# The low part of each weight tile by an accumulating transfer instead of a subtraction on VectorE

## The chip, the core and the metric

The kernel runs on one core of a Trainium2 chip. A core has engines that work side by side and each take their own instructions in order: TensorE (PE; its weight loads are shown as PEld), VectorE (DVE), ScalarE (ACT), GpSimd (POOL) and SyncE (SP), which here only starts transfers. Sixteen DMA engines move data between the main memory and the on-chip memory, and inside the latter. The metric is the time of one execution on the device in microseconds (us).

## The reference

One inference step of two layers for a prompt of 512 tokens and a sample of 64 tokens, 1024 features, all in float32. Layer 0 mixes by attention with forget gates and by a gated linear recurrence, layer 1 by a gated product over chunks of 128 tokens; each is followed by a feed-forward block of 2 x 2816 columns with a causal convolution of width 3. The products with weights are most of the work:

```
q, k, v, f, xb, gb = split(x @ w_in_e)            # 1024 x 2568
y = concat(attention(q, k, v, f), gelu(gb) * rg_lru(xb)) @ w_out_e
x = LN(ALPHA * x + y)
h = causal_dwconv(x @ ffn_w_up, ffn_conv_w)       # 1024 x 5632
g, u = split(h);  x = LN(ALPHA * x + (gelu(g) * u) @ ffn_w_down)
# layer 1: z = gelu(x @ w_in_o); u, v = split(z); y = (u * mixed(LN(v))) @ w_out_o; LN; the same FFN
```

## The kernel before

All 576 tokens stay on the chip, features on the partitions (`x`, eight blocks of 128). To multiply float32 values at the rate of float32r, a weight tile W and the activations X are each cut into a high part (the value rounded to float32r) and a low part (the rest), and each product is three matmuls: high x high, high x low, low x high (`triplet`, lines 293 to 295). The activations' parts are `xh`/`xl` or `hh`/`hl`.

The weights come as 188 tiles ("units", 128 partitions x up to 1040 columns, mostly 512 KB), in a fixed list. For each one, SP loads a raw tile (`raw`, four buffers, line 141). Then `split_part` makes the parts: ScalarE copies the raw tile into the high part (`whiA` or `whiB`, line 164), and VectorE subtracts high from raw into the low part (`wloA`/`wloB`, line 165). Pool A holds four units; pool B, which is open during the feed-forward blocks, four more. A unit is 8 blocks x 2 halves of the tokens x 3 = 48 matmuls, each with 288 columns.

The order of the work is written out by hand: no scheduler moves it. `need(units)` splits what is missing; after a unit's last matmul `retire` frees its slot and `pump(2)` splits up to two more units (`split_next`), and after each split the next raw load is issued (`dma_next`, at most four loads ahead). So in one engine's queue a split stands where the pump stands in the program, behind the evictions of the unit before it.

Three places differ from the steady stream:

- The start. The first two units are loaded and split in two pieces each, between the transposes of the input tokens (`x_in`, lines 511 to 513). POOL first starts 17 small loads (lines 247, 252, 528, 531).
- The ends of a mixer and of a feed-forward block (`tail_units`): the last four units run with one half of the tokens after the other, and pumps run inside the first half, while POOL and VectorE add up the sums for the layer norm (`Norm.acc`, lines 391 and 407; the statistics are matmuls at line 422). The next sublayer's first four units (`first_group`) follow.
- The token-major products (`v_sweep`, `vf_run`), where the weight is the moving operand and a unit is used up in a shorter time.

Of the kernel before, what the change touches and what calls it, by code (L numbers as in the profile page):

```python
# [22 lines left out]
AF = mybir.ActivationFunctionType  # L23
OP = mybir.AluOpType
# [31 lines left out]
def stream_step(ctx, tc, I, O):  # L56
    nc = tc.nc
    PE, ACT, DVE, POOL = nc.tensor, nc.scalar, nc.vector, nc.gpsimd
# [14 lines left out]
    x = big.tile([128, 8, T], FT, name="x")  # L73
    xh = big.tile([128, 8, T], FR, name="xh")
    xl = big.tile([128, 8, T], FR, name="xl")

# [1 line left out]
    units = []  # L78

    def wunit(w, off, ncols, c0, k0, nk, slot):  # L80
# [81 lines left out]
    def split_part(u, i):  # L162
        c = slice(u.parts[i][0] * u.width, u.parts[i][1] * u.width)
        ACT.activation(u.hi[:, c], u.raw[:, c], AF.Copy)  # L164
        DVE.tensor_sub(u.lo[:, c], u.raw[:, c], u.hi[:, c])  # L165

    def pump(n=1):
        for _ in range(n):
# [3 lines left out]
    def need(us):  # L172
        while any(u.hi is None for u in us):
            assert split_next()

    def retire(us):
        for u in us:
            live[u.slot] -= 1

# [1 line left out]
    later = []  # L181

    def defer(n, fn):
# [14 lines left out]
        while later:  # L198
            later.pop(0)[1]()

# [1 line left out]
    mones = consts.tile([128, 128], FT, name="mones")  # L202
    DVE.memset(mones, 1.0 / D)
    e0s, e0 = opened("ev0", side="left")
# [64 lines left out]
        nc.sync.dma_start(t[2], dram(s, l * 2 * 2 * DFF, [[128, 88], [1, 128]]))  # L269
        rowsF[l] = t  # L270

# [1 line left out]
    ps = {}  # L273

    def open_main():
        es, p = opened("psmain", side=None, space=bass.MemoryType.PSUM)
        ps["es"], ps["p"], ps["mm"] = es, p, ("mm", 6)
# [5 lines left out]
    def auxbank():  # L283
        return ps["p"].tile([128, 512], FT, name="aux", bufs=2)
# [31 lines left out]
    def seq(us, h, l, post, ks=None, hooks=None):  # L316
        for i, u in enumerate(us):
            need([u])
            for half in range(2):
                sweep([u], half, h, l, lambda _, hf, b, i=i: post(i, hf, b), ks=ks, hooks=hooks)  # L320
                hooks = None
            retire([u])
            pump(2)
# [14 lines left out]
        retire(us)  # L338
        pump(2)

# [1 line left out]
    lnp = {}  # L342

    class Norm:
        """Statistics of x = alpha * x + update about a per-token shift (the mean of the first 256 features)."""

        def __init__(self, g, b, first, halves=HALF, nb=96):
            self.g, self.b, self.first, self.halves, self.nb = g, b, first, halves, nb
# [126 lines left out]
                    at[2]: lambda: self.scale(half, 0, 4), at[3]: lambda: self.scale(half, 4, 8)}  # L475

    def tail_units(us, norm):
        """Output units 2..7 of a sublayer; the last four run one half of the tokens after the other."""
        seq(us[0:1], hh, hl, lambda i, hf, b: norm.post(2, hf, b), hooks={4: norm.shift})
        seq(us[-5:-4], hh, hl, lambda i, hf, b: norm.post(3, hf, b))  # L480
        us = us[-4:]
        need(us)
        post = lambda i, hf, b: norm.post(4 + i, hf, b)
        sweep(us, 0, hh, hl, post, hooks={c: pump for c in (3, 11, 19)})
        sweep(us, 1, hh, hl, post, hooks=norm.hooks(0))
        retire(us)
# [7 lines left out]
            retire(us[i:i + 2])  # L494
            pump(2)

    # =====================================================================
    # layer 0, even mixer
    # =====================================================================
    open_main()  # L500
    # the clock of TensorE rises after some microseconds of work: give it some while the first rows come in
    bk = auxbank()
    for _ in range(7):
        PE.matmul(bk[:, :128], mones, mones, start=True, stop=True)
# [43 lines left out]
    first = [E["xb0"], E["xb1"]]  # L548
# [18 lines left out]
    retire(first)  # L567
    pump(2)

    # per-channel vectors and the forget gates  # L570
    bk = auxbank()
    PE.transpose(bk[:, :112], rows0, ident[:112, :112])
    DVE.tensor_copy(vec, bk[:, :112])

    def log_sigmoid(z, w, name):
        """min(z, 0) - log(1 + e), e = exp(-|z|), the logarithm by the series of atanh(e / (2 + e)); z is overwritten."""
        e, t = e0.tile([128, w], FT, name=name + "e"), e0.tile([128, w], FT, name=name + "t")
        r = ev.tile([128, w], FT, name=name)
        DVE.scalar_tensor_tensor(e, z, -1.0, z, op0=OP.mult, op1=OP.max)
        ACT.activation(e, e, AF.Exp, scale=-1.0)  # L580
        DVE.tensor_scalar(t, e, 2.0, None, op0=OP.add)
        DVE.reciprocal(t, t)
        DVE.tensor_mul(e, e, t)
        DVE.tensor_mul(t, e, e)
        DVE.tensor_scalar(r, t, 1.0 / 19, None, op0=OP.mult)
        for d in (17, 15, 13, 11, 9, 7, 5, 3):
            DVE.scalar_tensor_tensor(r, r, 1.0 / d, t, op0=OP.add, op1=OP.mult)
        DVE.scalar_tensor_tensor(r, r, 1.0, e, op0=OP.add, op1=OP.mult)
        DVE.tensor_scalar(z, z, 0.0, None, op0=OP.min)
        DVE.scalar_tensor_tensor(r, r, -2.0, z, op0=OP.mult, op1=OP.add)  # L590
        return r
# [33 lines left out]
        seq([E[f"gb{j}"]], xh, xl, lambda _, hf, b: gb_post(j, hf, b))  # L625
        vecF_prep(j)

    # gates of the recurrence
    NXH = ((0, 290), (290, NX))
    for s, (dst, bias) in enumerate(((rr, "rg_ba"), (ii, "rg_bx"))):  # L630
        for j in range(4):
# [33 lines left out]
    for j in range(2, 4):  # L665
# [4 lines left out]
                p = 2 * (j - 2) + a  # L670
                PE.transpose(bk[:, 256 * a + 128 * t:256 * a + 128 * t + 128], ck[:, t, p * 128:(p + 1) * 128], ident)
        DVE.tensor_copy(ckT[:, 2 * j - 4:2 * j - 2, :], bk.rearrange("p (a c) -> p a c", a=2))
    # v, token-major
    vt = ev.tile([128, 5, 512], FT, name="vt")

    def v_sweep(us, post):
# [14 lines left out]
        for t in range(5):  # L691
            post(t, 128 if t < 4 else TS, banks[t])

    # the columns of v and of the forget gates lie side by side: two runs of 260
    lsz = e0.tile([128, 40], FT, name="lsz")
    DVE.memset(lsz, 0.0)

# [37 lines left out]
    nc.sync.dma_start(dram(O[3], 0, [[512, 128], [128 * 512, 4], [1, 512]]), vt[:, :4])  # L735
    nc.sync.dma_start(dram(O[6], 0, [[512, TS], [1, 512]]), vt[:TS, 4])

    # cumulative log forget values as rows: cached | new of the sample | prompt
    nb = e0.tile([8, 832], FT, name="nb")
    b0, b1 = auxbank(), auxbank()  # L740
    for t in range(4):
# [24 lines left out]
    def q_tiles(p):  # L766
        qh[p] = at.tile([128, TP - 128], FR, name="qh", bufs=3)
        ql[p] = at.tile([128, TP - 128], FR, name="ql", bufs=3)
# [7 lines left out]
        DVE.tensor_copy(kT[:, p, a:b], bk[:, :H2])  # L776

    def q_post(p, half, bk):
        """Scaled queries: the first tile of the prompt and the sample in float32, the rest as two float32r parts."""
        a, b = HALF[half]  # L780
        if half == 0:
            q_tiles(p)
        f0, f1 = (0, 128) if half == 0 else (TP, T)
        h0, h1 = (128, b) if half == 0 else (a, TP)
        hi, lo = qh[p][:, h0 - 128:h1 - 128], ql[p][:, h0 - 128:h1 - 128]
        ACT.activation(hi, bk[:, h0 - a:h1 - a], AF.Copy, scale=0.125)
        ACT.activation(qT[:, p, f0:f1], bk[:, f0 - a:f1 - a], AF.Copy, scale=0.125)
        DVE.scalar_tensor_tensor(lo, bk[:, h0 - a:h1 - a], 0.125, hi, op0=OP.mult, op1=OP.subtract)
# [41 lines left out]
    ats, at = opened("at", side="right")  # L830
# [4 lines left out]
    retire([E["k1"]])  # L835
    ps["es"].close()

# [1 line left out]
    aes, ap_ = opened("psatt", space=bass.MemoryType.PSUM)  # L839
    ps["p"], ps["mm"] = ap_, ("fil", 2)  # L840

# [190 lines left out]
    open_main()  # L1032
    tail_units(E["out"][2:8], n1)

    # =====================================================================
    # gated conv FFN
    # =====================================================================
    def ffn(layer, prev, norm):
        up, down = Fs[layer]
        V = vecF[layer]  # L1040
# [77 lines left out]
    wes["es"].close()  # L1118
    wpool["B"] = None

    # =====================================================================
    # layer 1, gated spatial mixing
    # =====================================================================
    oes, op = opened("odd", side="right")

    def u_post(m, half, bk):
# [113 lines left out]
    n4 = Norm(None, None, False, HALF4, 128)  # L1240
    dl = ffn(1, n3, n4)

# [1 line left out]
    fes, fp = opened("fin", side="right")  # L1244
    gB2 = fp.tile([128, D], FT, name="gB2")
    bB2 = fp.tile([128, D], FT, name="bB2")
# [123 lines left out]
```

## Time and profile before

| | |
|---|---|
| time, median of 2 runs | 1321.01 us (1320.17 to 1321.86) |
| profiled execution: span from first to last instruction | 1319.8 us; the profile tells no other time for it, so the runs stand beside the span |
| TensorE busy, matmul / weight load | 1290.8 us (98%) / 1256.0 us (95%) |
| VectorE, ScalarE, POOL busy | 768.4 us (58%), 483.1 us (37%), 398.2 us (30%) |
| granted TensorE clock, mean | 0.987 of full speed |
| transfers | 113.8 MB, 28.9% of the sixteen DMA engines' time on the hardware queue, 0.2% on the software queue |

A busy share is a mean over stages with different limits. Times are counted from the span's start. "Idle before, releaser" in a group means how long an engine sat idle ahead of such an instruction and what ended most of that. Instructions that only issue a transfer, wait or branch are not counted as busy, and SP's are shown as SPq.

### The profile page before, as it was taken

The numbers are of one execution on the slowest core, as the hardware profiler recorded it, in microseconds if no ns is written. First come the engines' busy times: TensorE is split into PE (matmuls) and PEld (weight loads), VectorE is DVE, ScalarE is ACT, GpSimd is POOL, SyncE is SP. The second block draws the span as 40 slices with busy tenths as digits, with TensorE's granted clock in tenths as the row PEclk, the third lists the DMA queues.
The fourth block names the chain that finished last, engine by engine and source line by source line (L and its number), as shares of the span: only waits on it lengthen the run. The fifth ranks groups of instructions, "written<-read, shape, count | busy, mean of one in ns | idle before, by whom it ended". The sixth has DMA issues, their size and how long they took to land. (4 is left out here: it accounts for less than half of the span.)

```text
span 1319.8 us, 23538 instructions
## 1 busy us (share of the span) xinstructions
PE 1290.8 (98%) x9567; PEld 1256.0 (95%) x9567; DVE 768.4 (58%) x1294; ACT 483.1 (37%) x936; POOL 398.2 (30%) x603
## 2 busy tenths in 40 slices
PE   8999999999999999999999998999999999999995
PEld 8999888999999999999999788999999999999995
DVE  4557777777543555355564348777653465445556
ACT  4553554445421332234334242444431233223331
POOL 3322222763200221022183025565320122012234
PEclk9999999999999999999999998999999999999997
DMA  9316221314232223322312412314323222322112
GB/s 234 113 33 199 79 84 41 97 47 144 83 96 80 74 74 94 97 75 71 94 38 68 139 50 73 96 33 128 113 80 96 78 66 81 97 86 64 43 36 72
DMA packets 192017, 113.80 MB, mean 86 GB/s; under 512 B 4221, under 2 KB 184733, under 8 KB 191909
## 3 DMA queue, kind: packets, MB, share of 16 engines
q1 hardware_dynamic: 191300, 111.95, 28.9%
q8 instruction: 75, 1.23, 0.4%
q0 software_dynamic: 608, 0.35, 0.2%
q14 instruction: 34, 0.27, 0.1%
HBM read 107.07 MB, written 5.22 MB: 85 GB/s over the span
## 5 line engine op out<-in xcount | busy, mean ns | idle before, releaser
L293 PE MATMUL mm<-xh,whiA 128*128 128x288 f32 (+2 forms) x960 | 285.4, 297 | 1.6 <-ACT xh L512 1.6
L295 PE MATMUL mm<-xh,wloA 128*128 128x288 f32 (+2 forms) x960 | 283.7, 296 | 1.4 <-DVE wloA L165 1.4
L294 PE MATMUL mm<-xl,whiA 128*128 128x288 f32 (+2 forms) x960 | 283.9, 296 | 0.5 <-DVE xl L513 0.5
L1064 DVE SCALAR_TENSOR_TENSOR y<-hb,vecF,y 128x578 f32<-128x578 f32 x176 | 146.5, 834 | 193.3 <-POOL y L1062 190.2
L1062 POOL TENSOR_SCALAR y<-hb,vecF 128x578 f32<-128x578 f32 x88 | 81.6, 928 | 557.5 <-issue 546.2
L293 PE MATMUL mm<-xh,whiB 128*128 128x288 f32 x768 | 226.5, 295 | 0.0
L295 PE MATMUL mm<-xh,wloB 128*128 128x288 f32 x768 | 226.4, 295 | 0.0
L294 PE MATMUL mm<-xl,whiB 128*128 128x288 f32 x768 | 226.2, 295 | 0.0
L165 DVE TENSOR_TENSOR wloA<-raw,whiA 128x1024 fp32r<-128x1024 f32 (+3 forms) x118 | 141.3, 1211 | 110.4 <-ACT whiA L164 109.8
L293 PEld LDWEIGHTS mm<-xh,whiA 128*128 128x128 f32 x960 | 181.3, 189 | 2.5 <-ACT xh L512 1.8
L295 PEld LDWEIGHTS mm<-xh,wloA 128*128 128x128 f32 x960 | 181.1, 189 | 1.6 <-DVE wloA L165 1.6
L294 PEld LDWEIGHTS mm<-xl,whiA 128*128 128x128 f32 x960 | 181.2, 189 | 0.7 <-DVE xl L513 0.7
L293 PE MATMUL mm<-hh,whiA 128*128 128x288 f32 (+2 forms) x576 | 171.5, 298 | 0.1
L294 PE MATMUL mm<-hl,whiA 128*128 128x288 f32 (+2 forms) x576 | 170.4, 296 | 0.8 <-DVE hl L1202 0.7
L295 PE MATMUL mm<-hh,wloA 128*128 128x288 f32 (+2 forms) x576 | 170.0, 295 | 0.0
L164 ACT ACTIVATE whiA<-raw 128x1024 fp32r<-128x1024 f32 (+3 forms) x118 | 119.5, 1025 | 133.7 <-PE mm L294 81.4
L293 PEld LDWEIGHTS mm<-xh,whiB 128*128 128x128 f32 x768 | 144.1, 188 | 0.0
L294 PEld LDWEIGHTS mm<-xl,whiB 128*128 128x128 f32 x768 | 144.1, 188 | 0.0
L295 PEld LDWEIGHTS mm<-xh,wloB 128*128 128x128 f32 x768 | 144.1, 188 | 0.0
L294 PEld LDWEIGHTS mm<-hl,whiA 128*128 128x128 f32 x576 | 108.8, 189 | 1.2 <-DVE hl L1202 1.2
L293 PEld LDWEIGHTS mm<-hh,whiA 128*128 128x128 f32 x576 | 108.8, 189 | 0.4 <-DVE x L361 0.4
L295 PEld LDWEIGHTS mm<-hh,wloA 128*128 128x128 f32 x576 | 108.6, 189 | 0.0
(330 smaller groups left out, 2374.1 us busy)
## 6 DMA issues: line engine op xcount, KB each, us to landing
raw<-in_ffn_w_up_dram SPq DMA_DIRECT2D x88, 512.0 KB
raw<-in_ffn_w_down_dram SPq DMA_DIRECT2D x32, 448.0 KB
raw<-in_ffn_w_down_dram SPq DMA_DIRECT2D x16, 512.0 KB
raw<-in_w_in_o_dram SPq DMA_DIRECT2D x16, 512.0 KB
raw<-in_w_in_e_dram SPq DMA_DIRECT2D x14, 512.0 KB
raw<-in_w_out_e_dram SPq DMA_DIRECT2D x8, 512.0 KB
raw<-in_w_out_o_dram SPq DMA_DIRECT2D x8, 512.0 KB
biasb<-nbd SPq DMA_DIRECT2D x4, 832.0 KB
```

The source lines that it names most:

```text
L164: ACT.activation(u.hi[:, c], u.raw[:, c], AF.Copy)
L165: DVE.tensor_sub(u.lo[:, c], u.raw[:, c], u.hi[:, c])
L293: PE.matmul(o, wh, h[:, k, a:b], start=first, stop=False)
L294: PE.matmul(o, wh, l[:, k, a:b], start=False, stop=False)
L295: PE.matmul(o, wl, h[:, k, a:b], start=False, stop=last)
L1062: POOL.tensor_scalar(y, t[:, 2:580], V[:, 88 + ct:89 + ct], V[:, 132 + ct:133 + ct], op0=OP.mult, op1=OP.add)
L1064: DVE.scalar_tensor_tensor(y, t[:, q:q + 578], V[:, 44 * q + ct:44 * q + ct + 1], y, op0=OP.mult, op1=OP.add)
```

## The change

`split_part` no longer subtracts. ScalarE writes the high part as before, and then a second copy of the raw tile with scale -1 into the low part's tile, rounded to float32r in the same way: the negated high part. Then POOL starts a transfer that adds the raw tile to what stands in the low part's tile, raw - high. All else is the same text, except that comments are gone; line 166 is new, so later lines move down by one.

```
 def split_part(u, i):
     c = slice(u.parts[i][0] * u.width, u.parts[i][1] * u.width)
     ACT.activation(u.hi[:, c], u.raw[:, c], AF.Copy)
-    DVE.tensor_sub(u.lo[:, c], u.raw[:, c], u.hi[:, c])
+    ACT.activation(u.lo[:, c], u.raw[:, c], AF.Copy, scale=-1.0)
+    POOL.dma_start(u.lo[:, c], u.raw[:, c], accum_op=OP.add)
```

The orders show where the new instructions stand. POOL at the start of the program, with what each waits for (DMASW are the eight semaphores by which its transfers tell that they have landed, DMAHW those of SP's loads). Before, from its tenth small load on:

```order
L252 DMA rows_120<-in_ln_mix_b_dram 16x128 [waits DMASW1_49]
L252 DMA rows_120<-in_ln_ffn_g_dram 16x128 [waits DMASW2_49]
L252 DMA rows_120<-in_ln_ffn_b_dram 16x128 [waits DMASW3_49]
L525 MEMSET wax 128x1024
L528 DMA wax<-in_rg_wa_dram 64x4x64 [waits DMASW4_49,Pool_49]
L528 DMA wax<-in_rg_wa_dram 64x4x64 [waits DMASW5_49]
L528 DMA wax<-in_rg_wx_dram 64x4x64 [waits DMASW6_49]
L528 DMA wax<-in_rg_wx_dram 64x4x64 [waits DMASW7_49]
L531 DMA lfc<-in_cache_logf_dram 128x2x8 [waits DMASW0_49]
L544 TENSOR_SCALAR xc<-x,vec 128x579 [waits DVE_49,Activation_49]
```

And with the change, the same place:

```order
L529 DMA wax<-in_rg_wx_dram 64x4x64 [waits DMASW7_49]
L532 DMA lfc<-in_cache_logf_dram 128x2x8 [waits DMASW0_49]
L166 DMA wloA<-raw 128x512 [waits DMAHW2_49,DMASW1_49,Activation_49]
L166 DMA wloA<-raw 128x512 [waits DMAHW3_49,DMASW2_49,Activation_49]
L166 DMA wloA<-raw 128x512 [waits DMAHW5_49,DMASW3_49,Activation_49]
L166 DMA wloA<-raw 128x512 [waits DMAHW6_49,DMASW4_49,Activation_49]
```

The four accumulating transfers of the first two units stand behind all small loads; the first waits for the semaphore DMASW1 that `rows<-in_ln_mix_b` updates. ScalarE's order at the same place, before (`xh` are the evictions of the input's transposes):

```order
L512 ACTIVATE xh<-mm 128x4x128 x2
L164 ACTIVATE whiA<-raw 128x512
L512 ACTIVATE xh<-mm 128x4x128 x2
L164 ACTIVATE whiA<-raw 128x512
L512 ACTIVATE xh<-mm 128x4x128 x2
L164 ACTIVATE whiA<-raw 128x512 x2
```

and with the change:

```order
L513 ACTIVATE xh<-mm 128x4x128 x2
L164 ACTIVATE whiA<-raw 128x512
L165 ACTIVATE wloA<-raw 128x512
L513 ACTIVATE xh<-mm 128x4x128 x2
L164 ACTIVATE whiA<-raw 128x512
L165 ACTIVATE wloA<-raw 128x512
L513 ACTIVATE xh<-mm 128x4x128 x2
L164 ACTIVATE whiA<-raw 128x512
L165 ACTIVATE wloA<-raw 128x512
L164 ACTIVATE whiA<-raw 128x512
L165 ACTIVATE wloA<-raw 128x512
```

Each high part is now followed by the negated copy; the second unit's copies still stand behind the third input tile's evictions. POOL at the end of layer 0's mixer (`s1r` and `a` are the norm's sums), before:

```order
L391 TENSOR_TENSOR a_2690<-a_2690,sq 128x288
L407 TENSOR_TENSOR s1r_2700<-s1r_2700,x 128x288
L407 TENSOR_TENSOR s1r_2695<-s1r_2695,x 128x288 x3
L407 TENSOR_TENSOR s1r_2700<-s1r_2700,x 128x288
L432 TENSOR_TENSOR sb<-sb,nhalf 96x3
```

and with the change:

```order
L392 TENSOR_TENSOR a_2718<-a_2718,sq 128x288
L408 TENSOR_TENSOR s1r_2728<-s1r_2728,x 128x288
L166 DMA wloA<-raw 128x1024
L166 DMA wloB<-raw 128x1024 x2
L408 TENSOR_TENSOR s1r_2723<-s1r_2723,x 128x288
L166 DMA wloB<-raw 128x1024
L408 TENSOR_TENSOR s1r_2723<-s1r_2723,x 128x288
L166 DMA wloB<-raw 128x1024
L408 TENSOR_TENSOR s1r_2723<-s1r_2723,x 128x288
L408 TENSOR_TENSOR s1r_2728<-s1r_2728,x 128x288
L433 TENSOR_TENSOR sb<-sb,nhalf 96x3
```

Five issues now stand between POOL's additions, each behind the landing of its raw tile and two copies on ScalarE.

## Rows read from the trace of the kernel before

**Rows 1.** The page, its first line and part 1: the span and each engine's busy time.

```profile
span 1319.8 us, 23538 instructions
...
PE 1290.8 (98%) x9567; PEld 1256.0 (95%) x9567; DVE 768.4 (58%) x1294; ACT 483.1 (37%) x936; POOL 398.2 (30%) x603
```

**Rows 2.** Waits of TensorE: who waited, for whom, us in total, times, longest.

```profile
PE mm L1183 <- DVE vo L1175: 5.3, 1, 5.3
...
PE aux L422 <- DVE s1r L407: 2.6, 3, 1.1
...
PE mm L295 <- DVE wloA L165: 1.4, 1, 1.4
```

**Rows 3.** Groups: the split on ScalarE (mean ns) and VectorE (min/median/max ns).

```profile
L164 ACT ACTIVATE whiA<-raw 128x1024 fp32r<-128x1024 f32 x94 | 97.7, 1054 | 132.8 <-PE mm L294 81.4 <-PE mm L688 44.4 <-PE mm L711 6.3
...
L165 DVE TENSOR_TENSOR wloA<-raw,whiA x118: 680/1221/2122, 8.7 to 1231.6; 128x1024 fp32r<-128x1024 f32 x94, 128x896 fp32r<-128x896 f32 x16, 128x512 fp32r<-128x512 f32 x4, 128x1040 fp32r<-128x1040 f32 x4
L165 DVE TENSOR_TENSOR wloB<-raw,whiB x72: 1083/1219/1834, 241.9 to 1257.1; 128x1024 fp32r<-128x1024 f32 x56, 128x896 fp32r<-128x896 f32 x16
```

**Rows 4.** Windows: stretch, busy us (x) of PE, PEld, DVE, ACT, POOL; PEclk, DMA share, GB/s.

```profile
400.00:460.00 60.00, 60.00 (x455) 60.00 (x455) 26.50 (x34) 16.95 (x32) 10.45 (x24) 1.00 0.26 76
116.00:124.00 8.00, 8.00 (x62) 8.00 (x62) 4.27 (x9) 4.12 (x7) 0.00 (x0) 1.00 0.83 303
```

**Rows 5.** Timeline, steady stretch: start, us, engine, line, one tile's split and first use.

```profile
425.74 1.06 ACT L164 ACTIVATE whiB<-raw 128x1024 fp32r<-128x1024 f32 x1
...
469.90 0.29 PE L295 MATMUL mm<-xh,wloB 128*128 128x288 f32 x1
```

**Rows 6.** Timeline and one window of the start: POOL, ScalarE, VectorE, TensorE.

```profile
8.89 0.49 POOL L252 DMA_DIRECT2D rows<-in_ln_mix_b_dram  x1 [0.47 <-DMA rows<-in_rg_conv_w_dram]
...
14.32 0.75 POOL L531 DMA_DIRECT2D lfc<-in_cache_logf_dram  x1
...
8.07 0.63 ACT L164 ACTIVATE whiA<-raw 128x512 fp32r<-128x512 f32 x1 [0.86 <-DMA raw<-in_w_in_e_dram]
...
8.73 0.69 DVE L165 TENSOR_TENSOR wloA<-raw,whiA 128x512 fp32r<-128x512 f32 x1 [0.79 <-ACT whiA L164]
...
10.33 0.42 PE L295 MATMUL mm<-xh,wloA 128*128 128x256 f32 x1
...
0.00:16.00 16.00, 12.67 (x68) 11.97 (x69) 7.55 (x18) 7.17 (x12) 11.08 (x23) 0.89 0.95 246
```

**Rows 7.** DMA issues of POOL: KB each, median us from issue to landing.

```profile
rows<-in_ln_mix_b_dram POOLq DMA_DIRECT2D x1, 8.0 KB, 6.8
...
out_dram<-ls POOLq DMA_DIRECT2D x1, 16.0 KB, 2.2
out_dram<-ls POOLq DMA_DIRECT2D x1, 2.0 KB, 1.6
```

**Rows 8.** Timeline of the handoff after the mixer, layer 0; last row: layer 1.

```profile
239.70 1.04 ACT L164 ACTIVATE whiA<-raw 128x1024 fp32r<-128x1024 f32 x1
...
248.81 1.04 ACT L164 ACTIVATE whiB<-raw 128x1024 fp32r<-128x1024 f32 x1
...
240.81 1.86 POOL L407 TENSOR_TENSOR s1r<-s1r,x 128x288 f32<-128x288 f32 x1
...
251.62 0.89 POOL L407 TENSOR_TENSOR s1r<-s1r,x 128x288 f32<-128x288 f32 x1 [2.22 <-DVE x L363]
...
253.25 0.67 PE L422 MATMUL aux<-mones,s1r 128*96 128x1 f32 x6 [0.55 <-DVE s1r L407]
...
859.94 0.89 POOL L407 TENSOR_TENSOR s1r<-s1r,x 128x288 f32<-128x288 f32 x1 [2.22 <-DVE x L363]
```

**Rows 9.** Windows behind two waits of TensorE, columns as in rows 4.

```profile
799.00:805.00 6.00, 6.00 (x28) 5.88 (x29) 4.26 (x5) 0.00 (x0) 0.32 (x1) 0.50 0.76 207
806.00:812.00 6.00, 6.00 (x49) 6.00 (x48) 5.79 (x6) 1.79 (x3) 4.77 (x4) 1.00 0.19 54
864.00:867.00 3.00, 3.00 (x15) 2.98 (x15) 2.43 (x7) 0.53 (x2) 2.75 (x4) 0.50 0.00 0
```


## The prediction

> **What bounds the kernel now.** I read the busy shares first: TensorE is busy for 1290.8 of 1319.8 us [rows 1]. The two runs shown have a median of 1321.01 us, so 1.2 us lie outside the span; I add every term below to 1321.0. Then TensorE's waits: the longest is 5.3 us, and the one wait for a low part in the whole run is 1.4 us [rows 2]. So no VectorE subtraction that the change takes away is waited for, except once. What the change can win is bounded by TensorE's idle time, under 30 us, and the 1.4 us are all of it that hangs on the removed line. What it can lose is the lead of the weight stream over TensorE.
>
> That lead is uneven. In the steady stretches it is large: the high part of the tile split at 425.74 us is first needed, as a low part, at 469.90 us [rows 5], 44 us later. One tile is 48 matmuls; 455 matmuls in 60 us make 6.33 us a tile [rows 4]. At the start and where a sublayer's last units run, the lead is a few us. The prediction is about those places.
>
> **The change, part by part.**
>
> *VectorE loses 190 subtractions* (118 + 72, median 1.22 us [rows 3]), some 227 us of work. VectorE is at 58% [rows 1], and TensorE waits for this line once: a gain of 0 to 1.4 us. I take 0, since that wait stands where the low part will come later still.
>
> *ScalarE gains 190 copies* of the high part's shape, 1.05 us each [rows 3], some 195 us, which lifts it from 37% to about 52%. In the steady stretches 44 us of lead hide 1 us. At handoffs it is one more microsecond before ScalarE's next operation.
>
> *POOL gains 190 DMA issues.* Each of its issues so far took 0.5 to 0.8 us [rows 6]; 0.8 for a 128-row one is my value, 150 us in all, on an engine at 30%. That is not a bound. But POOL runs in order, and an issue now waits on POOL for the copy on ScalarE, which waits for the raw tile's landing. What stands behind it waits too.
>
> *The transfer itself.* The trace has no accumulating transfer, so I bound it. A plain raw tile of 512 KiB takes 1.79 us of the sixteen engines: 0.26 of 60 us for 60 us at 76 GB/s [rows 4]. The faster end is the stretch with long rows: 0.83 of 8 us at 303 GB/s is 1.44 us per 512 KiB [rows 4]. An accumulate must also read what it adds to, so the slower end is twice the raw tile's cost, 3.6 us. I take 2.5 us, the middle: it is near both a pass and a half and two passes of the long-row price (2.2 and 2.9), and the accumulate's rows are long (4 KiB). Beside the raw stream, TensorE's pace leaves 6.33 x 0.74 = 4.7 us of transfer time per tile, so at 2.5 us the engines go to about 65% and stay off the path. To this comes the fixed part, from issue to landing: 2 us where the queue was quiet (1.6 and 2.2 for small ones), 6.8 us at the start, where the engines were 0.95 busy [rows 6, 7].
>
> The Trainium skill ("Collectives: The Full Stack", Part 3) says that a reducing transfer runs at half the copy's rate, not for its adder but because it reads two sources. No run here shows it yet; worked out from its 31 GB/s per engine, halved, 512 KiB would take an estimated 2.1 us, and the sum below would be some 7 us smaller.
>
> *The start: +12 us.* Today the first low part is ready at 9.4 us, and TensorE uses it at 10.33 us [rows 6]. In the changed order the first accumulate stands on POOL behind all of its seventeen set-up DMAs. The last of them starts at 14.32 and takes 0.75 us; eight completion semaphores go round, so the accumulate also waits for the tenth set-up DMA, issued at 8.89 us and landing 6.8 us later, at 15.7 us [rows 6, 7]. From there another 6.8 us, the price of software DMAs in this very stretch: 22.5 us, against 10.33, is +12.2. Bounds: 2.2 us to landing and half a tile at 1.44 give 18.6 (+8.3); 6.8 us and half a tile at 3.6 on top give 24.3 (+14).
>
> Here the Trainium skill ("DMA: Bandwidth & Descriptors", Anatomy of one DMA — SWDGE) would give less: a fixed 2.0 us plus bytes over 436 GB/s, an estimated 2.6 us for this half tile. By that rule the term would be +8. The landings of this stretch speak against it.
>
> *The second unit: +3 us.* Its copies on ScalarE stand behind evictions of transposes that TensorE does only after the stalled matmul, so its accumulate can't use the stall. Today its matmuls need it 6.2 us after the first low part is used; it would land 3.9 us of work, two half-tile copies (1.3), an issue and 3.3 us later, some 9 us: +3, between 0 and +6.
>
> *Two handoffs, after the mixers of layers 0 and 1: +5 us each.* There, four units' splits are pumped while the sublayer's last units run, and the order now puts each accumulate between POOL's additions for the norm's sums. Today the last of these splits begins at 248.81, POOL's addition at 251.62, and TensorE's statistics run at 253.25 us with 0.5 us of wait [rows 8]. The raw tile of the last split uses the buffer that the split of 239.70 frees [rows 8]. Now that buffer is free only when its accumulate has landed: POOL has its additions done at 240.81 + 1.86 = 242.7, then 0.8 + 2 + 2.5 gives 248.0. Load 3.8 (1.79 and 2), two copies 2.1, issue 0.8: POOL reaches the addition at 254.7 instead of 251.62. The statistics are 3 us later, and the two tiles consumed before them (needed 6 us after their high part) add 2 us of short waits: +5, bounds +2 (1.44 and faster landing) and +8 (3.6). The second handoff shows the same POOL pattern, its addition at 859.94 us [rows 8].
>
> *TensorE's clock: +8 us.* After a wait of 5.3 us the granted clock was 0.50 in a 6 us stretch, which costs 3 us; after one of about 1 us, 0.50 in 3 us, which costs 1.5 [rows 2, 9]. I count 3 for the start's stall, and 5 for the two handoffs, one of which already pays 1.5 today. Bounds 3 and 15.
>
> *Smaller handoffs: +8 us.* At some six places (forget gates, attention, the two token-major sweeps, two other norms) ScalarE or POOL comes about 1 us later ahead of a consumer that already waits; I allow 1 us each and some clock. Bounds 0 and 15.
>
> Sum: 12 + 3 + 10 + 8 + 8 = 41; 1321 + 41 = **1362 us**.
>
> **The rivals.** *The lead hides nearly all.* Accumulates land like a quiet queue's small DMAs and move at 1.44 us. Then the start costs 8, the second unit 0, the handoffs 2 each, the clock 3, the rest 1: 1321 + 16 = 1337 us, not slower by the 2% (26 us, 1347 us) that a measurement of this kernel can tell. For it: 44 us of lead on most tiles, 70% of the transfer time free. Against: the 6.8 us landings. It decides below about 3.5 us from issue to landing. Chance 0.22. The rule of the Trainium skill on software transfers, quoted above, would put the landing of a half tile on this side.
>
> *The sixteen transfer engines become the bound.* If the accumulate costs more than 4.7 us of them per tile, each tile needs more than TensorE's 6.33 us. At 6 us, 188 tiles x (1.79 + 6) = 1465 us, with the start some 1480. Nothing in the trace shows a transfer that slow for long rows, but nothing shows this kind at all. Chance 0.13.
>
> *Faster.* ScalarE and VectorE are both off TensorE's path, and 2% would be more than all waits of TensorE together. It would need fewer low-clock stretches and the waits on VectorE gone: at best 1321 - 10 = 1311. By over 2%: 0.02. That the change doesn't do what it says is out: the built order has 190 such transfers and no subtraction.
>
> **How the numbers follow.** My forecast, a moderate loss from start and handoffs, has 0.63. Its own range goes with the bounds: 12 becomes 8 to 14, 3 becomes 0 to 6, 10 becomes 4 to 16, 8 becomes 3 to 15, 8 becomes 0 to 15, so 1336 to 1387. A price of 3.6 to 4.7 us, where bursts of splits no longer fit, and the saturated case lie above. The range 1336 to 1430 leaves out about 0.07 below and 0.12 above. Faster by over 2% 0.02; within 2% 0.23 (the hidden case and the low edge of mine); slower 0.75.
>
> **What would show it.** The changed profile should have TensorE waiting for the first low part until 20 to 24 us; about twice the bytes in transfer, with the engines' share in steady stretches at 0.5 to 0.7 instead of 0.26; steady stretches with TensorE as full as now; longer waits of the statistics matmuls after POOL's additions in the two handoffs; and more low-clock stretches. A steady stretch with TensorE idle and the transfer share near 1 would be the saturated case. A first low part used before 19 us would make the forecast too high.

## The result, and the profile after

The changed kernel takes 1373.98 us (median of 2 runs, 1372.13 to 1375.83) against 1321.01: a ratio of 1.040, interval 1.037 to 1.044. It is slower by 53.0 us (48 to 58 by the interval); 41 were forecast. The profiled execution of the changed kernel has a span of 1374.1 us and took 1375.83.

The page of the changed kernel, its first line, part 1 and two queues of part 3 (q0 carries POOL's transfers, q1 SP's loads; packets, MB, share of sixteen engines), answers to [rows 1]:

```profile
span 1374.1 us, 23914 instructions
...
PE 1304.9 (95%) x9567; PEld 1268.5 (92%) x9567; DVE 555.7 (40%) x1104; ACT 654.4 (48%) x1126; POOL 513.5 (37%) x793
...
q0 software_dynamic: 27968, 96.87, 39.5%
q1 hardware_dynamic: 191300, 111.95, 27.8%
```

VectorE lost 213 us (227 forecast), ScalarE gained 171 (195), POOL 115 (150): the work moved as announced, by somewhat less, and none of the three is near a bound. POOL's issues are counted as busy here, unlike those of SP; one of the 190 took 0.88 us (0.8 forecast). The cost of one accumulating transfer comes out of q0: 0.395 x 1374.1 us of all sixteen engines for 96.87 MB is 2.94 us for 512 KiB.

The waits of TensorE in the changed kernel (us in total, times, longest) answer to [rows 2]; all source lines stand one later than before:

```profile
PE mm L296 <- DMA wloA<-raw: 20.1, 4, 12.7
PE aux L423 <- DVE s1r L408: 10.2, 3, 4.7
PE mm L294 <- ACT hb L1057: 6.6, 2, 3.6
```

They are new or several times as long; the wait for `vo`, the longest before, grew only from 5.3 to 5.6. There are few long waits, not many short ones. To place them I compared, matmul for matmul (both kernels have 9567), when each starts in the two traces; its lag is how much later it starts in the changed kernel:

| stretch of the changed run | lag added, us | new waits in it, us |
|---|---|---|
| start, to 34 us | 16.1 | 12.7, 1.5; 2.8 instead of 1.6 |
| 34 to 261 us | -1.0 | 1.0; a wait of 1.4 us of before is gone |
| handoff after layer 0's mixer, 261 to 291 | 12.4 | 3.0; 4.5 instead of 0.55 |
| first units of layer 0's FFN, 350 to 366 | 4.5 | 2.95 |
| 366 to 890 us | 3.8 | 1.4 and shorter |
| handoff after layer 1's mixer, 890 to 919 | 10.1 | 2.9; 4.65 instead of 0.94 |
| first units of layer 1's FFN, 979 to 996 | 6.3 | 3.6 |
| the rest of the matmuls | 0.0 | |

That is 52.2 us; 1.9 more come behind the last matmul. Three kinds of place make 49 of the 52: the start, the two handoffs and the first units of the two FFNs. Behind the last matmul the first of POOL's closing `DRAIN` instructions is the longest of three, before and in the changed kernel (min/median/max in ns):

```profile
L1366 POOLq DRAIN  x3: 46/93/3273, 1313.5 to 1319.6; - x3
...
L1367 POOLq DRAIN  x3: 46/93/7472, 1365.8 to 1373.8; - x3
```

It takes 7.5 instead of 3.3 us, and now ends after SP's last waits instead of before them. In `e4_copy_and_dve_add`, where POOL starts no such transfer, it takes 3.3 us again; no run shows why it takes longer.

**The start.** POOL, TensorE and ScalarE in the changed kernel (start, us, engine, line; in brackets the idle time before it and what ended it) against [rows 6]:

```profile
14.43 0.74 POOL L532 DMA_DIRECT2D lfc<-in_cache_logf_dram  x1
16.50 1.88 POOL L166 DMA_DIRECT2D wloA<-raw  x2 [1.33 <-DMA rows<-in_ln_ffn_g_dram]
29.12 0.85 POOL L166 DMA_DIRECT2D wloA<-raw  x1 [10.75 <-ACT wloA L165]
...
23.58 0.58 PE L296 MATMUL mm<-xh,wloA 128*128 128x256 f32 x1 [12.73 <-DMA wloA<-raw]
32.52 0.38 PE L296 MATMUL mm<-xh,wloA 128*128 128x256 f32 x1 [1.51 <-DMA wloA<-raw]
```

The first low part is used at 23.58 us instead of 10.33. POOL could not issue its accumulate before 16.50 us, and 7.1 us pass from there to the matmul. The table's third wait, 2.8 instead of 1.6 us, is for an eviction on ScalarE that now stands behind a negated copy; TensorE came to it earlier than before, so that it puts the matmul back by only 0.5 us.

**The handoff.** ScalarE and TensorE in the changed kernel, at the place of [rows 8]:

```profile
260.52 0.43 ACT L403 ACTIVATE sq<-x 128x288 f32<-128x288 f32 x1
264.49 1.06 ACT L164 ACTIVATE whiB<-raw 128x1024 fp32r<-128x1024 f32 x1 [3.54 <-DMA raw<-in_ffn_w_up_dram]
265.45 1.04 ACT L165 ACTIVATE wloB<-raw 128x1024 fp32r<-128x1024 f32 x1
266.40 0.42 ACT L403 ACTIVATE sq<-x 128x288 f32<-128x288 f32 x1
272.52 1.06 ACT L164 ACTIVATE whiB<-raw 128x1024 fp32r<-128x1024 f32 x1 [5.70 <-DMA raw<-in_ffn_w_up_dram]
...
264.68 0.60 PE L296 MATMUL mm<-hh,wloA 128*128 128x288 f32 x1 [2.96 <-DMA wloA<-raw]
277.06 1.12 PE L423 MATMUL aux<-mones,s1r 128*96 128x1 f32 x6 [4.46 <-DVE s1r L408]
```

ScalarE stands still twice, 3.5 and 5.7 us, ahead of a split whose raw tile has not come; the squares of the norm (`sq`) stand behind that split, and the additions to the norm's sums behind those. Why the tile has not come, SP's waits from 250 to 276 us show (L141 is the load of a raw tile):

```profile
SPq L141 <- DMA wloA<-raw: 15.8, 2, 9.0
SPq L141 <- DMA wloB<-raw: 10.1, 3, 6.2
```

The load waits for a buffer, and each such wait ends when an earlier accumulate lands. POOL's transfers of the same 26 us (KB each, median us from issue to landing) took 6 to 8 us:

```profile
wloB<-raw POOLq DMA_DIRECT2D x4, 512.0 KB, 8.3
wloA<-raw POOLq DMA_DIRECT2D x2, 512.0 KB, 6.0
```

Over the whole run the median of the 512 KB ones is 5.7 us (`wloA`) and 5.9 (`wloB`). Layer 1 repeats these waits of ScalarE and TensorE within 0.5 us.

**The first units of the FFN.** The same, with evictions (`hb`) in place of squares:

```profile
351.57 1.06 ACT L164 ACTIVATE whiA<-raw 128x1024 fp32r<-128x1024 f32 x1 [3.90 <-DMA raw<-in_ffn_w_up_dram]
...
353.47 0.39 ACT L1057 ACTIVATE hb<-mm 128x288 f32<-128x288 f32 x1
...
353.92 0.61 PE L294 MATMUL mm<-xh,whiB 128*128 128x288 f32 x1 [2.95 <-ACT hb L1057]
```

**Steady stretch and clock.** Windows of the changed kernel, columns as in [rows 4]:

```profile
12.00:33.00 21.00, 7.91 (x44) 7.71 (x45) 2.67 (x4) 4.63 (x9) 6.74 (x9) 0.59 0.86 167
400.00:460.00 60.00, 60.00 (x455) 60.00 (x454) 13.05 (x25) 24.38 (x30) 13.79 (x23) 1.00 0.86 185
264.00:285.00 21.00, 15.85 (x84) 15.59 (x85) 6.66 (x19) 6.79 (x11) 7.74 (x10) 0.68 0.97 220
275.00:285.20 10.20, 8.14 (x39) 8.10 (x40) 5.76 (x17) 2.18 (x6) 6.06 (x8) 0.50 0.82 189
```

The first is the stall of the start. In the steady stretch (the second) TensorE is as full as before, 455 matmuls in 60 us. In the handoff the transfer engines are at 0.97. Around the end of the wait of 4.46 us (at 277.06) the granted clock is 0.50 (1.2 GHz) for 10.2 us, from 275.0 to 285.2.

### The profile page after: what moved, and what is told of

Same layout as the page of the kernel before. It is cut to its first block, busy times and chain, and to the rows that moved or that the text cites. A ratio compares the mean times of both kernels' runs of the same rounds, so it can differ in the third digit from the quotient of the medians.

```text
span 1374.1 us, 23914 instructions
## 1 busy us (share of the span) xinstructions
PE 1304.9 (95%) x9567; PEld 1268.5 (92%) x9567; DVE 555.7 (40%) x1104; ACT 654.4 (48%) x1126; POOL 513.5 (37%) x793
## 3 DMA queue, kind: packets, MB, share of 16 engines
q0 software_dynamic: 27968, 96.87, 39.5%
## 5 line engine op out<-in xcount | busy, mean ns | idle before, releaser
L166 POOL DMA_DIRECT2D wloA<-raw x118 | 103.1, 888 | 393.6 <-ACT wloA L165 267.0
L296 PEld LDWEIGHTS mm<-xh,wloA 128*128 128x128 f32 x960 | 181.6, 189 | 14.7 <-DMA wloA<-raw 14.6
L296 PE MATMUL mm<-hh,wloA 128*128 128x288 f32 (+2 forms) x576 | 173.0, 300 | 5.9 <-DMA wloA<-raw 5.9
L294 PE MATMUL mm<-hh,whiA 128*128 128x288 f32 (+2 forms) x576 | 174.4, 303 | 0.2 <-DVE x L362 0.2
L166 POOL DMA_DIRECT2D wloB<-raw x72 | 63.2, 877 | 214.3 <-ACT wloB L165 113.7
L165 ACT ACTIVATE wloA<-raw 128x1024 fp32r<-128x1024 f32 (+3 forms) x118 | 120.3, 1020 | 0.0
L1063 POOL TENSOR_SCALAR y<-hb,vecF 128x578 f32<-128x578 f32 x88 | 75.1, 856 | 107.0 <-issue 102.7
```

The lines of the kernel that those rows point to most:

```text
L165: ACT.activation(u.lo[:, c], u.raw[:, c], AF.Copy, scale=-1.0)
L166: POOL.dma_start(u.lo[:, c], u.raw[:, c], accum_op=OP.add)
L294: PE.matmul(o, wh, h[:, k, a:b], start=first, stop=False)
L296: PE.matmul(o, wl, h[:, k, a:b], start=False, stop=last)
L1063: POOL.tensor_scalar(y, t[:, 2:580], V[:, 88 + ct:89 + ct], V[:, 132 + ct:133 + ct], op0=OP.mult, op1=OP.add)
```

## The experiments

Edits are against the changed kernel unless a line says otherwise; ratios are to the kernel before. In three of them low parts are different numbers, and the time is read for the order and the transfers alone: in `e3_source_high` they are zero, in `e9_start_and_source` zero for all units but the first two, in `e6_plain_copy` they are the raw tile. The two runs of the changed kernel lie 3.7 us apart, the four runs of `e1` 6.9 and those of `e3` 6.2, so a gain against the changed kernel is good to some 3 us. Where a lag is told below, it is that of the profiled execution, over the same matmuls as in the table's stretches.

**The first two units by VectorE.**

```
         ACT.activation(u.hi[:, c], u.raw[:, c], AF.Copy)
+        if len(u.parts) > 1:
+            DVE.tensor_sub(u.lo[:, c], u.raw[:, c], u.hi[:, c])
+            return
```

> The changed kernel, but the first two units (four half tiles) get their low parts by the VectorE subtraction again; the other 186 keep the accumulating transfer. My theory (the first low part is late since its transfer stands behind POOL's set-up loads and lands slowly): TensorE's 12.7 us wait at 23.6 us goes, and with it the low-clock stretch from 12 to 29 us; 13 to 17 us of the 53 us come back, so 1357 to 1361 us, and the rest of the trace is as in the changed kernel, shifted. Rival (the start is bound by the transfer engines, which the other accumulates load as well): the wait moves to the third unit, and less than 6 us come back.

Measured: 1361.00 us, ratio 1.031 (1.028 to 1.033). TensorE's waits:

```profile
PE aux L426 <- DVE s1r L411: 9.6, 3, 6.5
PE mm L299 <- DMA wloA<-raw: 9.0, 3, 4.1
PE mm L297 <- ACT hb L1060: 6.2, 2, 3.2
```

The wait of 12.7 us is gone and 13.0 us of time with it; the two other kinds stay. Of the 9.0 us for low parts 2.24 are new, at the third unit, which now gets the first accumulate: the rival's sign, but a small wait. The start is a cause of its own, of about 13 us; 40 remain.

**The first accumulates ahead of five set-up loads.** The clearing of `wax`, its four loads and that of `lfc` are issued behind the four accumulates of the first two units.

```
-    POOL.memset(wax, 0.0)
...
-    POOL.dma_start(lfc, dram(I["cache_logf"], 0, [[8, 128], [1024, 2], [1, 8]]))
...
+    POOL.memset(wax, 0.0)
...
+    POOL.dma_start(lfc, dram(I["cache_logf"], 0, [[8, 128], [1024, 2], [1, 8]]))
```

> The changed kernel, but the last five of POOL's seventeen set-up loads and the memset before them stand behind the first four accumulating transfers instead of ahead of them. Theory (POOL's queue): the first accumulate is issued at about 11 instead of 16.5 us and lands 6 to 7 us later; TensorE's first wait falls from 12.7 to 6 to 8 us, and 4 to 7 us come back: 1367 to 1370 us. Rival (the transfer engines' backlog of raw tiles and tokens decides when it lands): first low part still at about 23 us, the time within 3 us of 1374.

Measured: 1368.69 us, ratio 1.037 (1.035 to 1.038). POOL and TensorE:

```profile
11.02 1.87 POOL L166 DMA_DIRECT2D wloA<-raw  x2 [0.33 <-ACT whiA L164]
...
19.40 0.58 PE L296 MATMUL mm<-xh,wloA 128*128 128x256 f32 x1 [8.40 <-DMA wloA<-raw]
```

Issued 5.5 us earlier, used 4.2 us earlier. So 4 of the 12.7 us were the place behind the set-up loads; 8.4 us are the transfer from issue to use, which this order on POOL did not take away.

**The norm's sums all on VectorE.** If POOL's additions wait behind issues, this frees them.

```
-                (DVE if m > 2 else POOL).tensor_add(self.a2[half], self.a2[half], sq)
+                DVE.tensor_add(self.a2[half], self.a2[half], sq)
...
-                POOL.tensor_add(self.a1[half], x[:, 0, a:b], xm)
+                DVE.tensor_add(self.a1[half], x[:, 0, a:b], xm)
...
-                (DVE if m >= self.dve else POOL).tensor_add(self.a1[half], self.a1[half], xm)
+                DVE.tensor_add(self.a1[half], self.a1[half], xm)
```

> The changed kernel, but the additions for the norms' sums run all on VectorE instead of partly on POOL; POOL keeps the transfers' issues. My theory (at the two mixer handoffs POOL's additions stand behind issues that wait for raw tiles): the statistics matmuls' waits of 4.5 and 4.7 us fall below 1.5 us each, with less low clock behind them: 8 to 14 us faster than the changed kernel, 1360 to 1366 us. Rival (the handoff is late because of ScalarE, whose extra copies stand ahead of the squares): the waits stay above 3.5 us and the time within 4 us of 1374.

Measured: 1367.35 us, ratio 1.036 (1.034 to 1.038). ScalarE and TensorE at the handoff of layer 0:

```profile
269.82 1.06 ACT L164 ACTIVATE whiB<-raw 128x1024 fp32r<-128x1024 f32 x1 [5.19 <-DMA raw<-in_ffn_w_up_dram]
...
273.07 1.12 PE L423 MATMUL aux<-mones,s1r 128*96 128x1 f32 x6 [6.08 <-DVE s1r L408]
```

The wait of the statistics did not go; it grew from 4.46 to 6.08 us, with not one addition left on POOL and ScalarE still idle for 5.2 us ahead of a raw tile. My mechanism for the statistics falls; the time, 6.6 us under the changed kernel, fits neither my theory nor the rival. Most of it comes with the loss of the waits of 2.96 and 2.91 us for low parts: the two handoffs' lag is 16.5 instead of 22.5 us. Why these went shows on ScalarE. In the changed kernel a square waits 1.7 us (0.6 before) for POOL's addition `a`, which stands behind an issue there; the next split stands behind the square, and its accumulate behind the split. The first two lines are of the changed kernel, the third is the same issue in this run:

```profile
254.48 0.45 ACT L403 ACTIVATE sq<-x 128x288 f32<-128x288 f32 x1 [1.71 <-POOL a L392]
257.12 0.87 POOL L166 DMA_DIRECT2D wloA<-raw  x1 [0.40 <-ACT wloA L165]
...
254.91 0.86 POOL L166 DMA_DIRECT2D wloA<-raw  x1 [1.71 <-ACT wloA L165]
```

It comes 2.2 us earlier (0.9 of them by the shorter time up to there) and lands 5.4 instead of 7.5 us after its issue. So POOL's additions do cost something in a handoff, but through a low part.

**The raw buffer let go early.** The same transfers, of the same bytes, but they read the high part, so the raw tile is free after ScalarE's two copies.

```
-        POOL.dma_start(u.lo[:, c], u.raw[:, c], accum_op=OP.add)
+        POOL.dma_start(u.lo[:, c], u.hi[:, c], accum_op=OP.add)
```

> The changed kernel, but the transfer adds the high part instead of the raw tile, so the low part comes out as zero; everything else, the bytes included, is the same, only the raw buffer is free after ScalarE's two copies and not after the landing. My theory (in the refills after the handoffs four raw buffers are held some 6 us longer, raw loads come late, ScalarE waits for one and the evictions behind it stall TensorE): the waits at 354 and 983 us (3.0 and 3.6 us) vanish and the statistics' waits shrink by 2 us or more each: 8 to 18 us faster than 1374. Rival (the doubled traffic slows the raw loads): the two waits stay above 2 us and the time within 4 us of 1374.

Measured: 1355.78 us, ratio 1.027 (1.025 to 1.029). Waits of TensorE:

```profile
PE mm L296 <- DMA wloA<-whiA: 23.1, 9, 11.7
...
PE mm L294 <- ACT hb L1057: 1.1, 2, 0.8
```

ScalarE at the handoff:

```profile
268.06 1.06 ACT L164 ACTIVATE whiB<-raw 128x1024 fp32r<-128x1024 f32 x1 [1.58 <-DMA raw<-in_ffn_w_up_dram]
```

SP's loads of raw tiles now wait for operations of ScalarE instead of a landing, and ScalarE's idle time at the handoff ahead of a raw tile, 3.5 and 5.7 us above, is one of 1.6 us. The statistics matmuls of the two handoffs no longer wait (of those in [rows 2] the 1.1 us of another place are left), and the evictions' 6.6 us went to 1.1: 18.2 us less time in all. The accumulates themselves were not faster: their median landing grew from 5.7 to 7.3 us. So in the handoffs and the first units of the FFNs it is mostly not the late low part that costs, but that the raw buffer stays shut meanwhile: their lag went from 33.3 to 1.1 us, though waits of 2.6 and 3.1 us for low parts remain in the handoffs. Elsewhere 9 us of lag were added, with the slower accumulates and nine waits for low parts instead of four.

**Both causes undone together**, `e1` and `e3` in one kernel.

> Both edits at once: the first two units by VectorE, and all other transfers add the high part instead of the raw tile (their low parts come out as zero), so that raw buffers are free after ScalarE's copies. If start and raw-buffer hold are two separate causes, their gains add: 1374 - 13 - 18 = 1343 us, within 5 us (the rest being low parts that land late after short leads). If they are one (the stalled start makes the later rush), clearly less comes back: 1350 us or more.

Measured: 1342.45 us, ratio 1.016 (1.014 to 1.018). The two gains, 13.0 and 18.2 us, add to 31.2; it gained 31.5. They are separate causes; that the sum fits to 0.3 us, with gains good to 3, is chance. Of the 21 us left, TensorE's waits show

```profile
PE mm L299 <- DMA wloA<-whiA: 10.4, 6, 2.8
...
PE mm L691 <- DMA wloA<-whiA: 3.3, 1, 3.3
```

13.7 us in places where a tile is split only just ahead of its use, under the longer landings of this edit.

**The hold without the dependence.** The kernel *before*, unchanged in its arithmetic, with an accumulating transfer of each raw tile into a scratch in main memory that nobody reads. Here TensorE never needs a transfer's result.

```
         DVE.tensor_sub(u.lo[:, c], u.raw[:, c], u.hi[:, c])
+        POOL.dma_start(drams.tile([128, 1040], FT, name="side", bufs=8)[:, c], u.raw[:, c], accum_op=OP.add)
```

> The kernel before, with its VectorE subtraction, and beside it each raw tile is also added by an accumulating transfer of the same shape from POOL into a scratch in main memory that nobody reads. So the bytes, POOL's issues and the longer hold of the raw buffers are there, but neither the wait for a low part nor ScalarE's second copy. My theory, as it stands after the first four runs (the start costs 16 us by the late first low part; the handoffs and the refills behind them cost some 30 us because four raw buffers are held until the transfer has landed): no wait for a low part at the start, but ScalarE waiting for raw tiles ahead of the norm's squares, the statistics matmuls waiting 3 us or more at both mixer handoffs, and 1338 to 1352 us. Rival (the low parts' own lateness is what costs, everywhere): 1321 to 1328 us.

Measured: 1353.21 us, ratio 1.025 (1.024 to 1.027), a little over the span that I gave. ScalarE and TensorE at the handoff:

```profile
262.70 1.06 ACT L164 ACTIVATE whiB<-raw 128x1024 fp32r<-128x1024 f32 x1 [9.04 <-DMA raw<-in_ffn_w_up_dram]
...
270.24 1.12 PE L423 MATMUL aux<-mones,s1r 128*96 128x1 f32 x6 [9.71 <-DVE s1r L408]
```

No wait for a low part at the start, none in the FFN's first units, but the statistics wait 9.7 us, twice as long as in the changed kernel; the landing here has a median of 7.6 us. So a transfer whose result nobody uses costs 32 us. Of the lag, 21.3 us lie in the two handoffs, where SP's loads wait for its landing, and 8.0 between start and the first handoff, with waits for VectorE of 2.5 and 1.9 us, which I did not trace further. This run adds the traffic together with the hold; that the hold is what counts in the handoffs rests on `e3_source_high`, where the traffic stayed and the waits went.

**A plain copy in its place**: same source, target, order and bytes, no addition.

```
-        POOL.dma_start(u.lo[:, c], u.raw[:, c], accum_op=OP.add)
+        POOL.dma_start(u.lo[:, c], u.raw[:, c])
```

> The changed kernel, but the transfer copies the raw tile over the low part's tile instead of adding to it, so the low part is wrong; issues, order and semaphores are the same. My theory: the add costs transfer time because the destination is read too; a packet of 4 KiB takes half as long, the software queue's share falls from 39% to about 20%, the landing from 5.7 to some 4 us, and with buffers free earlier 8 to 15 us come back: 1359 to 1366 us. Rival (the price is that of any software transfer, the add is free): share within 5 points of 39% and the time within 4 us of 1374.

Measured: 1348.25 us, ratio 1.021 (1.019 to 1.023), 26 us under the changed kernel, more than I expected. POOL's queue and the landing of a 512 KB transfer:

```profile
q0 software_dynamic: 27968, 96.87, 22.5%
...
wloA<-raw POOLq DMA_DIRECT2D x94, 512.0 KB, 3.3
```

TensorE's waits:

```profile
PE mm L296 <- DMA wloA<-raw: 13.2, 2, 11.8
PE aux L423 <- DVE s1r L408: 7.6, 3, 3.3
```

0.225 x 1347.9 us for 96.87 MB is 1.64 us for 512 KiB, against 2.94 with the addition: a ratio of 1.8. The landing is 3.3 instead of 5.7 us. The first wait is nearly the same (11.8 instead of 12.7), so there the addition hardly counts; at the handoffs the statistics' wait shrinks with the landing (to 3.2 and 3.3 us), and the FFN's waits go.

**No transfer at all**: ScalarE's negated copy, then an addition on VectorE.

```
-        POOL.dma_start(u.lo[:, c], u.raw[:, c], accum_op=OP.add)
+        DVE.tensor_add(u.lo[:, c], u.raw[:, c], u.lo[:, c])
```

> The changed kernel, but VectorE adds the raw tile to the negated high part in place; no transfer. This leaves ScalarE's 190 further copies as the only change against the kernel before. My theory (the copies cost little, the transfer all): 1321 to 1329 us, the same as before by 2%, most of it at the start and the handoffs. Rival (ScalarE, in order, is what delays the evictions): 1335 us or more, with TensorE waiting for ScalarE's evictions.

Measured: 1345.58 us, ratio 1.019 (1.017 to 1.020). The time is that of the rival, though its sign is absent: no wait for the evictions `hb`. Both handoffs still wait (5.65 and 6.03 us). ScalarE there:

```profile
253.66 0.45 ACT L403 ACTIVATE sq<-x 128x288 f32<-128x288 f32 x1 [1.72 <-DVE x L364]
254.01 1.04 ACT L164 ACTIVATE whiB<-raw 128x1024 fp32r<-128x1024 f32 x1
254.96 1.05 ACT L165 ACTIVATE wloB<-raw 128x1024 fp32r<-128x1024 f32 x1
257.72 0.44 ACT L403 ACTIVATE sq<-x 128x288 f32<-128x288 f32 x1 [1.72 <-DVE x L364]
```

One round takes 4.06 us (253.66 to 257.72); before it took 3.11 (245.35 to 248.46). Here VectorE's addition follows ScalarE's two copies, its next `x` stands behind that addition, and ScalarE's next square needs that `x`: the second copy lies in a ring. With the transfer VectorE isn't in the ring, and `e3_source_high`, with the same copies, has no such wait. 14.7 of the 24.7 us of lag lie in the two handoffs. So this run doesn't measure the copies' share in the changed kernel; I had chosen it for that, and it doesn't tell.

**Accumulating only where the lead is long**: tiles 48 to 91 and 140 to 183 of 188, the middle and end of the two FFNs; the others by VectorE. It is the version that the findings point to.

```
+        n = units.index(u)
+        if not (48 <= n < 92 or 140 <= n < 184):
+            DVE.tensor_sub(u.lo[:, c], u.raw[:, c], u.hi[:, c])
+            return
```

> A mixed kernel: the accumulating transfer only for the 88 tiles that the feed-forward blocks read in mid stream (positions 48 to 91 and 140 to 183 of the list, all with more than 33 us between split and first use before), the VectorE subtraction for the other 100. My theory (where the lead is large the transfer is free, and all of the loss is in start, handoffs and refills): 1318 to 1326 us, the same as before, with no new wait of TensorE over 1 us. Rival (the added traffic and copies cost a little on every tile): a loss in proportion, 88/188 of what start and handoffs leave, 1335 us or more.

Measured: 1323.73 us over 10 runs, ratio 1.002 (1.001 to 1.003). TensorE's longest waits:

```profile
PE mm L1188 <- DVE vo L1180: 5.3, 1, 5.3
...
PE aux L427 <- DVE s1r L412: 2.5, 3, 1.1
```

They are those of before. With 88 accumulates, near half, the kernel takes 3 us more, and in the profiled execution TensorE has no share in that: the last matmul starts at 1308.7 us (1308.6 before), and POOL's closing `DRAIN` takes 7.9 instead of 3.3 us. They save nothing either: VectorE's time isn't waited for there.

**Only fifty tiles spared**: units 0 and 1, and the 24 around each handoff (24 to 47, 116 to 139).

```
+        n = units.index(u)
+        if n < 2 or 24 <= n < 48 or 116 <= n < 140:
+            DVE.tensor_sub(u.lo[:, c], u.raw[:, c], u.hi[:, c])
+            return
```

> The changed kernel with VectorE's subtraction for 50 tiles only, the first two and those at positions 24 to 47 and 116 to 139 (the two mixer handoffs and the refills behind them); 138 tiles keep the transfer. If the loss sits in those places, four fifths or more of the 53 us come back: 1323 to 1332 us, no wait of the statistics matmuls above 1.5 us, none of TensorE for evictions. If it is spread over the tiles, 1350 us or more.

Measured: 1326.43 us, ratio 1.004 (1.003 to 1.006). 47.6 of the 53.0 us are back with 138 accumulates still in place, and of the waits for a transfer the longest is this:

```profile
PE mm L300 <- DMA wloA<-raw: 1.5, 1, 1.5
```

So the loss sits where the table puts it; the run doesn't tell the copies from the transfers, since the fifty tiles are spared both. No version is faster than the kernel before.

## Why the prediction was right, point by point

The sign held, and the time lies 12 us above the 1362 forecast, in a range that was 94 us wide (1336 to 1430). By its steps:

- *A gain of 0 to 1.4 us from VectorE, taken as 0.* The wait of 1.4 us is gone and the lag falls by 1.0 us in that stretch. Right, and as small as said.
- *The start, +12.* The first low part comes 13.25 us later. The accumulate was issued at 16.50 (15.7 forecast), released by a small load's landing as forecast (the trace names the one behind the one that I named), and was used 7.1 us later (6.8). Right. The Trainium skill ("DMA: Bandwidth & Descriptors", Anatomy of one DMA — SWDGE) would have a half tile land in an estimated 2.6 us and make the term +8; this trace doesn't agree, with 7.1 us from issue to use in a stretch whose transfer engines are 0.86 busy, nor does the run with the earlier issue (8.4 us).
- *The second unit, +3 (0 to 6).* A wait of 1.51 us; lag +1.7. POOL stood 10.75 us for the copy, as forecast.
- *The price X, 2.5 us (1.44 to 3.6).* 2.94 us, and a landing of 5.7 instead of 4.5. The Trainium skill ("Collectives: The Full Stack", Part 3) has the reducing steps of a ring, which read two sources, at half the copy's rate; this case nearly agrees, with 1.64 us for the plain copy of the same bytes against 2.94. The estimate of 2.1 us worked out from its rate was too low, since the copy itself took longer than that rate gives. That the sum would then be some 7 us smaller is not worked out, and the handoffs' own bounds (+2 at 1.44 us, +5 at 2.5) give about 1 us each.
- *Steady stretches, share 0.5 to 0.7.* 0.86 (0.82 from 413 to 473 us): wrong, and it didn't matter. The price of 2.94 us makes 0.75 of it at the pace of 6.33 us a tile; the rest I did not follow. TensorE is as full as before, so even there the rival of saturation is not reached.
- *Two handoffs, +5 each (2 to 8).* New waits of 6.9 us (2.96 + 4.46 - 0.55) and 6.6. The place and about the size were right, **the mechanism half wrong**. The failed step is "POOL reaches the addition at 254.7": that POOL's late additions hold the statistics. With no addition on POOL the wait stays; what went, 6.0 of the 22.5 us of lag, went by the low parts. The other half, "now that buffer is free only when its accumulate has landed", is the cause, but the wait it makes bites on ScalarE: a split whose raw tile is late stands in ScalarE's order ahead of the squares. Freeing the buffer early took the wait away with slower accumulates; holding it, with the same bytes but without any use of the result, made it longer.
- *Clock, +8 (3 to 15).* Lag beyond the waits: 0.7 at the start (16.1 - 12.7 - 1.5 - 1.2), 12.4 - 6.9 and 10.1 - 6.6 in the handoffs, 4.5 - 2.95 and 6.3 - 3.6 in the FFNs: some 14 us, as TensorE's busy time grew by 14.1 at the same matmuls. I had 3 for the start and 5 for the handoffs, they took 0.7 and 9: mis-sized, near the upper bound in all.
- *Six smaller places, +8 (0 to 15).* In the stretches that hold them the lag grows by about 3. What I missed are the first units of the two FFNs: 2.95 + 3.6 us of waits, 11 us with the clock. Had I followed "the buffer is free only at the landing" to every place where ScalarE has both a split and an eviction that TensorE waits for, it would have been on the list. The allowance of 8 thus stood for 3 us in the places that I named and 6.6 in two that I had not: the sum came nearer than its reasons deserve.

Open are why POOL's closing `DRAIN` takes 4 us longer, the 8 us of lag that the unused transfer makes ahead of the first handoff, and the share of ScalarE's extra copies alone. A fifth raw buffer, the direct remedy, wasn't tried.

## What to carry to other kernels

When a computation is moved to a transfer, ask first how long its *source* is held: a buffer that a 0.7 to 1.2 us instruction let go stayed shut until a landing 6 to 8 us after the issue here, and letting it go early gave back 18 us, more than undoing the late result at the start (13). In the profiled executions it took 32 us of lag away at the places where the hold bit and added 9 elsewhere, where the transfers were slower. Then look which engine stands, in order, behind the next load into that buffer, since its other work is what comes late. And freeing an engine that nobody waits for gives nothing back, however many us of it are saved: 213 here.

## What the runs showed that I had not expected

- The addition in a transfer costs 1.8 times the plain copy in transfer time (2.94 against 1.64 us for 512 KiB) and 2.4 us in landing (5.7 against 3.3).
- Transfer engines at 0.86 for 60 us did not delay TensorE at all, where the lead was long.
- The new waits of 3 to 5 us came with stretches of 3.4 to 10.2 us at a granted clock of 0.50, which began up to 2.6 us before the wait's end; in the handoffs this cost two thirds as much again as the waits themselves (9 us beside 13.5).
- 88 accumulates in mid stream cost TensorE nothing. What the kernel with them lost lies behind the last matmul, where POOL's closing `DRAIN` takes 7.9 instead of 3.3 us.
